# Norm factors of the second mixer moved behind the output projection, in one kernel of a four-mixer block

## The chip, the cores and the metric

The kernel runs on one core of a Trainium2 chip. The metric is the device time of one execution in microseconds; lower is better.

## The reference

One block of a model: `x` (512 tokens x 1024) is normalised, projected by `w_in`, and the projected columns feed four mixers whose outputs, 512 channels each, are concatenated and projected back by `w_out`. Cut to what matters here, the second mixer (a chunked state-space mixer) ends with a norm over each of two groups of 256 channels:

```
h = _rmsnorm(x, norm_g[l])
p_fox, p_ssm, p_nsa, p_mem = _split(h @ w_in[l], ...)
...
yg = (y * jax.nn.silu(z)).reshape(B, S, SSM_GROUPS, GROUP_W // SSM_GROUPS)
return _rmsnorm(yg, norm_g.reshape(SSM_GROUPS, -1)).reshape(B, S, GROUP_W)
...
o = jnp.concatenate([fox, ssm, nsa, mem], axis=-1)
x = x + o @ w_out[l]
return _rmsnorm(x, final_norm_g)
```

`_rmsnorm` multiplies each token's group by `rsqrt(mean(y*y) + EPS)`, one factor for each token and group, and by a gain for each channel.

## The kernel before

All matrix products that need full precision are split in two float32r parts, high and low, and computed as three matmuls (`three`): high by high, high by low, low by high. Weights come from HBM in 75 tiles of 128x1024 in the order of the table `ORDER` (line 53): `load` issues the DMA of a tile into a ring of three buffers (`raw`), `split` makes its high part on ACT (`wh`) and its low part on DVE or POOL (`wl`), and `get` hands both to the matmuls.

Two kinds of work alternate on TensorE. The background is a list of generators in `ORDER`: projections of 128 columns (`tile_a`, eight steps of three matmuls of 512 columns, after a first step that only takes the weights), then a "sink" that moves the result out of PSUM with several ACT and DVE instructions. The pipes are the mixers (`fox`, `ssm`, `nsa`, `mem`, and the small `prep` and `cmp`), each cut into stages. Which goes when is written out by hand in the string `PLAN` (line 67): `.3` is three background steps, `L0` issues the next weight DMA, `W0` splits the next weight tile, `O1` splits one output tile of mixer 1, and a letter with a number is the next stage of a pipe (`f0` is the first stage of fox, `s4` the fifth of ssm). The string sets the order of instructions on each engine; semaphores set the times. `PICKS` says for each instruction that could go to several engines which one takes it (V DVE, A ACT, P POOL).

The second mixer works channel-major: in its stage `s3` a chunk of 128 tokens is a tile `yc` of 128 channels by 4x128 tokens, and its squares go to `sq`. `s4` sums the squares over channels with a matmul against ones (tile `pn`) and takes the power -1/2 on POOL (`rsr`), which gives a factor for each token in the partition direction. `s5` turns the factors into rows over all partitions with two fp32 matmuls against the identity (`bcast_rows`, tile `prs`) and multiplies `yc` by the gain and the rows into `of` with four DVE instructions. Later `split_o` makes the high and low parts `oh` and `ol`, and `out_proj(1, c)` multiplies them by the weights `wo1`: for each pair of token tiles it sums all four channel tiles f = 0 to 3 in one PSUM tile `po` for each token tile, and one DVE addition for each token tile brings the sum into `acc`. A loop over c covers the two halves of the 1024 outputs. The same function serves mixers 0 and 2; the last, mixer 3, has `out_last`, followed by the final norm.

PSUM has eight tiles of 128x512 for everything (`PS`). Every `PS` tile is taken again once its readers are done.

Of the kernel before, what the change touches and what calls it, by code (L numbers as in the profile page):

```python
# [67 lines left out]
    "p0.9W0.8L0.5W0.2L0p1W0.7L0L0.2W0.9L0L0.6W0.6W0f0f0f0.6L0L0.3f1.6W0.1W0.5f0L0.4f1.6W0f1.3L0f1L0.6W0.3"  # L68
    "f2.5L0.1f3.1f0f2f0f0f2.3W0W0f2.4f3f1.2f1.4f2f2f4.5f3.1f3W0f0f4f0L0.6f4.2f5.1f1L0.3f3.1W0L0.4W0f4f1f0"
    "f2f0f1.6L0L0.5f3f3.6W0W0f0.2f1f1f2.1f2.2f4f4.1W0f3f3s0.1f4f1f4f0f0f0f1f1f1f4f2f2.2f3.5L0L0.4f5f2f2.1"  # L70
    "f2f3f2.4W0W0.6f4L0L0f0L0f3c0.1W0.3f5.1f3f5f5f5f3.5W0.9.1f4f4f5.4f4f4O0f1f5f5L0.1s0s0.3L0f2s1s1.5W0.2"
# [1 line left out]
    "W0s3B0B0B0.2L0.3s4L0s4s4.1B0.1W0.9.6W0W0s5s5s5n0n0.7L0.2L0n1.3W0W0.2L0L0L0n0n1n0.1n1.3n2n2n2.8n1W0n3"
    "n0.1n1W0.5n2W0L0n3n4n4n2.4n0n0n3n5n5n3L0.8n1n1W0L0n4n0.2O1O1.2n2.3n3.3n2.2W0.1n3n0.1n0n0n1n1.3O1.3L0"
    ".1L0.3n2W0W0n5.2n1n1n0n0n4n4n4.4L0.1n2W0O1.7n1n1n3n4n2n2n3n3n2n0L0.2n3n3n0n5.5W0n5n3n2.4L0.1n5n3n0n4"
    "n4.1n5n5.4n0n1n4n4n0L0n1n1W0n2n0n2n4.3n1.1n2.3n5L0.4W0.3n5.4n2W0n5n5.3n1n1n3n0n0n0.8L0L0.1n3W0n2n1n1"
    ".4n3n3n3.3n1n4n4n4n4.1W0n5n2W0n5n5n5n0n0n0n0.3n1.1n4.1n2n2.1n2.2L0n3.3W0.9n3.1n1n3.2B0n4n4.2n0L0L0n2"
    ".3L0n4.1n4n1W0n1n2n5n5n3.1W0.2n5.3n0n0n3n1n3.8n2.1n0.3n0W0L0L0n2.5n2n1n5n1n4n4n4n3n1W0n3n3n0n2.2n2n1"
    "n4n4.1n3.3n4W0.9n2.3L0m0m0L0m0.2W0L0.3W0.2n1m1n5m1n5n5n5n4m1n2.2n5n5O2n5n3n3m2.1n2W0.4m2.1m3.1m2.1m3"
    "m3m4n4m0m0m0m0n5m4m4n3n5.1n3.1m5m5O2m1m1n4.1n4m2L0n4n5n5m2L0m1m3m6n5L0m2m5O2O2m3m3m0.2m4.1W0.4m4.5W0"  # L80
    "m4.3m5m5m5m1m1m2W0m6m6m2m3m3.1L0.1L0.3m4m4L0.2m6.4W0.4m6m6.1m5m5.1W0.2m6m6.2W0.9.9.9.9.1"
# [4 lines left out]
    "M": "VAAAVVVA",  # L86
    "Rk": "AVVAAVVV",
    "Rl": "VAAAAAVA",
    "ce": "PPVVVV",
    "ct": "AVAAVAVVAAVAVVVA",  # L90
    "kh0": "AVV",
    "kh1": "AVV",
    "ll": "PVPVPPVV",
    "m": "PVVPVPVV",
# [2057 lines left out]
```

## Time and profile before

| | |
|---|---|
| median of 3 runs | 511.45 us (511.14 to 514.05) |
| the profiled execution | 511.3 us, of which the span from first to last instruction is 509.5 us |
| TensorE (PE) busy | 496.4 us, 97% of the span, 2965 matmuls |
| DVE, ACT, POOL busy | 368.9, 297.3 and 164.4 us |
| mean granted TensorE clock | 0.997 |

A busy time counts how long instructions of the engine lasted; a matmul's record lasts longer than the distance to the next one, since matmuls are pipelined. So what a matmul takes of the engine's time is read from the distance of the starts of neighbours. An idle time is named after what ended it.

### The profile page before, as it was taken

How to read it: one execution, taken by the hardware profiler on the slowest of the kernel's cores; microseconds unless marked ns; L12 is line 12 of the kernel's file. 1: busy time of each engine (PE TensorE's matmuls, PEld its weight loads, DVE VectorE, ACT ScalarE, POOL GpSimd, SP SyncE). 2: the span in 40 equal slices, each digit the busy share in tenths (PEclk: the TensorE clock that was granted, in tenths of full speed). 3: DMA queues.
4: the chain of work that ended last, by engine and by line, in shares of the span. 5: the costliest groups of instructions: out<-in, count | busy, mean ns of one | idle time of the engine just before them, and what ended most of it. 6: DMA issues, size and time to landing. Idle time of an engine off the chain costs nothing.

```text
span 509.5 us, 8995 instructions
## 1 busy us (share of the span) xinstructions
PE 496.4 (97%) x2965; PEld 419.6 (82%) x2965; DVE 368.9 (72%) x981; ACT 297.3 (58%) x671; POOL 164.4 (32%) x113
## 2 busy tenths in 40 slices
PE   8999999989999999999899999999999999999995
PEld 5898877877788888888788888788888898898884
DVE  5486686667678688997988786787777786655644
ACT  5856366777545535664464776755756654664343
POOL 3594303030133103643653132340251220521532
PEclk9999999999999999999999999999999999999998
DMA  8791824526687679444345477777766776832213
GB/s 300 314 326 53 93 85 144 183 79 170 155 262 214 194 228 373 130 171 170 132 152 172 123 225 198 238 219 213 197 196 212 233 233 163 255 138 83 84 41 124
DMA packets 72446, 92.66 MB, mean 182 GB/s; under 512 B 26784, under 2 KB 50624, under 8 KB 72400
## 3 DMA queue, kind: packets, MB, share of 16 engines
q1 hardware_dynamic: 71968, 91.51, 58.5%
q10 hardware_dynamic: 432, 0.59, 0.3%
q8 instruction: 23, 0.38, 0.3%
q14 instruction: 23, 0.19, 0.1%
HBM read 73.68 MB, written 20.55 MB: 185 GB/s over the span
## 4 chain that ended last, share of the span: by engine, by line
PE 56%; DVE 19%; ACT 9%; DMA 6%; issue 5%; SPq 2%; POOL 2%; POOLq 0%; ACTq 0%; DVEq 0%
PE pj L360 25%; PE po L360 10%; PE pb L360 7%; PE pO L360 5%; PE pS L360 4%; ACT pN L360 3%; DMA raw<-in_wst 3%; DVE wl L360 2%; DVE fl L360 2%; SPq L360 2%; DVE pN L360 1%; DVE xs L360 1%; ACT pF L360 1%; DMA far<-fl 1%; DVE rs L360 1%
## 5 line engine op out<-in xcount | busy, mean ns | idle before, releaser
L360 POOL TENSOR_TENSOR wl<-raw,wh 128x1024 fp32r<-128x1024 f32 (+1 forms) x44 | 109.3, 2493 | 258.9 <-ACT wh L360 182.9
L360 PE MATMUL pj<-hh,wl 128*128 128x512 f32 x352 | 137.6, 391 | 3.5 <-POOL wl L360 2.8
L360 PE MATMUL pj<-hh,wh 128*128 128x512 f32 x352 | 138.5, 393 | 0.5 <-ACT wh L360 0.5
L360 PE MATMUL pj<-hl,wh 128*128 128x512 f32 x352 | 137.2, 390 | 0.0
L360 PEld LDWEIGHTS pj<-hh,wl 128*128 128x128 f32 x352 | 66.1, 188 | 19.1 <-POOL wl L360 3.6
L360 ACT ACTIVATE wh<-raw 128x1024 fp32r<-128x1024 f32 (+1 forms) x72 | 73.3, 1034 | 8.5 <-DMA raw<-in_wst 3.4
L360 PEld LDWEIGHTS pj<-hh,wh 128*128 128x128 f32 x352 | 66.1, 188 | 14.7 <-ACT wh L360 0.9
L360 PEld LDWEIGHTS pj<-hl,wh 128*128 128x128 f32 x352 | 66.1, 188 | 13.0
L360 ACT ACTIVATE pN<-pN,nm 128x128 f32<-128x128 f32 (+7 forms) x96 | 45.3, 473 | 37.5 <-DVE nm L360 36.3
L360 DVE TENSOR_TENSOR wl<-raw,wh 128x1024 fp32r<-128x1024 f32 (+1 forms) x29 | 37.8, 1310 | 4.6 <-ACT wh L360 4.1
L360 PE MATMUL po<-wh,oh 128*128 128x512 f32 x96 | 37.7, 393 | 0.0
L360 PE MATMUL po<-wh,ol 128*128 128x512 f32 x96 | 37.5, 390 | 0.0
L360 PE MATMUL po<-wl,oh 128*128 128x512 f32 x96 | 37.5, 390 | 0.0
L360 ACT ACTIVATE pF<-pF,nm 128x128 f32<-128x128 f32 (+3 forms) x32 | 17.8, 556 | 28.3 <-DVE nm L360 27.4
L360 DVE TENSOR_TENSOR acc<-acc,po 128x512 f32<-128x512 f32 (+1 forms) x33 | 21.1, 663 | 9.9 <-PE po L360 9.8
L360 DVE STREAM_TRANSPOSE fl<-pN 128x128 f32<-128x128 f32 (+3 forms) x64 | 27.9, 482 | 0.1
L360 DVE SCALAR_TENSOR_TENSOR rs<-sm,gat 128x3 f32<-128x3 f32 x32 | 6.6, 206 | 28.8 <-ACT pN L360 28.8
L360 ACT ACTIVATE pN<-pN,rs 128x128 f32<-128x128 f32 (+3 forms) x31 | 16.1, 544 | 12.9 <-DVE rs L360 12.9
L360 DVE CUSTOM_DVE_ANT_0 pN<-pS,bt 128x128 f32<-128x128 f32 (+5 forms) x80 | 22.1, 320 | 0.1
L360 DVE SCALAR_TENSOR_TENSOR xs<-x,cwh,xs 128x512 f32<-128x512 f32 x24 | 19.0, 790 | 4.0 <-ACT xs L360 3.4
L360 PEld LDWEIGHTS po<-wh,ol 128*128 128x128 f32 x96 | 18.0, 188 | 3.8
L360 PEld LDWEIGHTS po<-wl,oh 128*128 128x128 f32 x96 | 18.0, 188 | 3.6
(273 smaller groups left out, 1009.2 us busy)
## 6 DMA issues: line engine op xcount, KB each, us to landing
raw<-in_wst SPq DMA_DIRECT2D x73, 512.0 KB, 5.0
far<-fl SPq DMA_DIRECT2D x144, 64.0 KB, 2.1
pt<-far SPq DMA_DIRECT2D x36, 256.0 KB, 3.9
far<-fl SPq DMA_DIRECT2D x96, 48.0 KB, 1.7
pt<-far SPq DMA_DIRECT2D x24, 192.0 KB, 2.9
rows<-rv SPq DMA_DIRECT2D x4, 656.0 KB, 7.1
bt<-rows SPq DMA_DIRECT2D x4, 528.0 KB, 4.9
xn<-in_xn SPq DMA_DIRECT2D x4, 512.0 KB, 7.2
```

Of the source, the lines that this page charges most:

```text
L360: return f(*a, **k)
```

## The change

Stage `s5` of the second mixer is gone. `s4` writes its factors into a fixed tile `rn` (128 tokens by 4 chunks x 2 groups) and multiplies `yc` by the gain alone into `of`, in one instruction of 128x512 for each chunk, on the engine that `PICKS` names. In `out_proj(1, c)` the two groups of channels are summed apart: the matmuls of f = 0, 1 form one PSUM sum and those of f = 2, 3 another, and each is scaled by its column of `rn` and added into `acc` by one DVE instruction (`scalar_tensor_tensor`). The tables `ORDER`, `PLAN` and `PICKS` are new throughout; all tiles and stages but `s5` are in both. The diff, with `ORDER` whole and of `PLAN` and `PICKS` the lines that are spoken of:

```diff
 ORDER = (
-    ("bv", 0), ("bv", 1), ("bv", 2), ("bv", 3), ("bc", 0), ("bc", 1), ("bc", 2), ("fq", 0), ("xb", 6),
-    ("fk", 1), ("xb", 3), ("xb", 0), ("fk", 0), ("kc", 0), ("fk", 3), ("fk", 2), ("fq", 1), ("fq", 3),
-    ("fq", 2), ("fg", 0), ("vc", 0), ("xb", 1), ("z", 2), ("xb", 5), ("fg", 2), ("z", 3), ("xb", 7), ("fg", 3),
-    ("xb", 4), ("fg", 1), ("xb", 2), ("z", 1), ("z", 0), ("kw", 0), ("nq", 0), ("wo0", 0), ("wo0", 1),
-    ("ks", 0), ("nq", 2), ("mv", 0), ("mv", 1), ("mv", 2), ("mv", 3), ("nq", 1), ("mg", 3), ("wo0", 2),
-    ("wo0", 3), ("ng", 0), ("ng", 2), ("ng", 1), ("wo1", 0), ("wo1", 1), ("mk", 3), ("nq", 3), ("ng", 3),
-    ("wo1", 2), ("wo1", 3), ("mq", 0), ("mg", 0), ("mk", 2), ("mk", 0), ("mg", 1), ("mk", 1), ("mq", 1),
-    ("mq", 2), ("mq", 3), ("mg", 2), ("wo2", 2), ("wo2", 3), ("wo2", 0), ("wo2", 1), ("wo3", 0), ("wo3", 1),
+    ("bv", 0), ("bv", 1), ("bv", 2), ("bv", 3), ("bc", 0), ("bc", 1), ("bc", 2), ("xb", 6), ("fq", 0),
+    ("z", 3), ("xb", 3), ("fg", 0), ("fk", 0), ("xb", 0), ("kc", 0), ("fq", 3), ("fq", 1), ("fk", 2),
+    ("fk", 1), ("z", 2), ("xb", 1), ("fq", 2), ("z", 1), ("fk", 3), ("fg", 2), ("vc", 0), ("fg", 1), ("xb", 5),
+    ("xb", 7), ("xb", 4), ("xb", 2), ("fg", 3), ("nq", 0), ("z", 0), ("kw", 0), ("wo0", 0), ("wo0", 1),
+    ("nq", 2), ("ks", 0), ("mv", 0), ("mv", 1), ("mv", 2), ("mv", 3), ("nq", 1), ("ng", 0), ("wo0", 2),
+    ("wo0", 3), ("ng", 2), ("mg", 3), ("ng", 1), ("mk", 3), ("wo1", 0), ("wo1", 1), ("nq", 3), ("wo1", 2),
+    ("wo1", 3), ("ng", 3), ("mq", 2), ("mk", 1), ("mg", 0), ("mq", 3), ("mq", 0), ("mk", 0), ("mk", 2),
+    ("mq", 1), ("mg", 1), ("mg", 2), ("wo2", 0), ("wo2", 1), ("wo2", 2), ("wo2", 3), ("wo3", 0), ("wo3", 1),
     ("wo3", 2), ("wo3", 3),
 )
...
 PLAN = (
...
-    "f5W0.2f5f5f3f3s2f5c1f4f5s3f4f5B0f5O0c2O0W0.1O0s1.9.3s0L0W0.3s2s2c3s3L0s3.2L0L0.5s4s1.9.2W0W0.3s2L0s5"
...
+    "L0p0.9.1W0.9.1W0.6L0.3L0L0.8W0W0L0.4W0.2L0.9.4W0.3p1f0L0f0f0f0.9.1f1f1W0.7f2L0f2s0.1f3.2f1W0W0L0.2L0"
+    "L0.2f2.3f0.2f4.3f1.3f2W0.1f3f3.1f2f4O0.2f3.1f5.1f5f5.1f1.7L0.3L0f2f5f3f2.1f5.2f5f4f5f3W0.1W0.2f3.1W0"
+    "c0f4.5s0.8s1s1f5f4f4L0L0f5f5.5f4W0c1s2.1s0f5c2O0s2L0O0O0s1.9L0W0.1s3s3c3W0s2.6s3s4B0s4s1.2W0.6s2.3L0"
+    ".2W0.3s3.3B0B0L0W0.5B0B0.5L0.1L0.1W0.3L0.7W0s4s4W0n0.2L0n1L0L0.4W0.4W0n0n0.6n2L0.3L0n1n1n2n2.3O1.3W0"
+    ".3L0n2n5.1W0n3W0.2n2n2n1n1O1W0n0n3.2B0n1.2n2.4n0L0L0n2.7n1.2n3.4n5n5.1n2n5n3W0n4n4n4L0L0n1n4n2W0n3n3"
+    "n5n1.2n3.2n1n4L0.7m0m0.3n5.3n4.2W0n1m0m0n2n2m0n4n4n3n3m1m1n5n5n5n5m2m2W0m1.8m3m3m2m1.1m4O2n4.1O2O2n2"
...
 PICKS = {
...
-    "pF": "VVVVVVVAVAVVVVAVAAVVVVVAAVVVAVVV",
-    "pN": "AVVVAAVVAVAAAAVAVAVAVAAAVVVVVAAVAAVAVVAAAVVVAVAVAAAVAVVAVVAAVVVV",
-    "xde": "VVV",
-    "xp": "VVPVVVVV",
-    "yc": "PVVVVVVVVVVPVVVP",
+    "of": "VPVV",
+    "pF": "AAAVVVVVAAAAVVAAVAAVAAVAVVAVVAVV",
+    "pN": "VAAAAVAAAVAAVAAAAAAVAVAVVAAVVAAVAAVVAAVAAVAVVVVVVAVAVAAAVAAAVVAV",
+    "xde": "VPV",
+    "xp": "PPPVPVVP",
+    "yc": "PPVPVVVVPPVPPPPV",
...
@@ -530,7 +531,7 @@
 
 CONSTS = {"ones": [128, 128], "umask": [128, 128], "vcm": [96, 128], "w2": [128, 2, 64], "sp": [128, 4, 16],
           "nv": [128, 4, 296], "dA": [128, 32], "cst": [128, 776], "nhalf": [128, 8], "cbh": [128, 8], "rx": [128, 4],
-          "gat": [128, 4, 24], "x0": [128, 632], "cwh": [128, 32], "nacs": [128, 32],
+          "rn": [128, 8], "gat": [128, 4, 24], "x0": [128, 632], "cwh": [128, 32], "nacs": [128, 32],
           "dte": [128, 32], "decR": [128, 32]}
 
 
@@ -1088,6 +1089,8 @@
         tk = slice(f * 128, (f + 1) * 128) if mixer == 1 else slice(t * 128, (t + 1) * 128)
         three(p, (hi[:, tk], lo[:, tk]), (w_[0][:, cs], w_[1][:, cs]), f == ends[0], f == ends[1], 512)
 
+    rn = C1("rn")
+
     def out_proj(mixer, c):
         if not acc:
             load_acc()
@@ -1099,7 +1102,7 @@
                 for x in range(2):
                     t = 2 * t2 + x
                     for f in (2 * i, 2 * i + 1):
-                        first = f == (0 if t2 == 0 else 2)
+                        first = f % 2 == 0 if mixer == 1 else f == (0 if t2 == 0 else 2)
                         hi, lo = o_hl[mixer, t if mixer == 1 else f]
                         yield max(clock.ready([hi, lo, *w_[i]]), clock.free_banks(1) if first else 0.0)
                         if first:
@@ -1107,10 +1110,16 @@
                                 p = []
                             p.append(PS("po"))
                         cs = slice(f % 2 * 512, f % 2 * 512 + 512)
-                        out_mm(p[x], mixer, t, f, w_[i], cs, (0, 3) if t2 == 0 else (2, 1))
+                        out_mm(p[x], mixer, t, f, w_[i], cs,
+                               (2 * i, 2 * i + 1) if mixer == 1 else (0, 3) if t2 == 0 else (2, 1))
                 if t2 == 1:
                     done(w_[i])
-            for x in range(2):
+                for x in range(2) if mixer == 1 else ():
+                    t = 2 * t2 + x
+                    a = acc[t][:, 512 * c:512 * c + 512]
+                    V.scalar_tensor_tensor(out=a, in0=p[x], scalar=rn[:, 2 * t + i:2 * t + i + 1], in1=a,
+                                           op0=OP.mult, op1=OP.add)
+            for x in range(2) if mixer != 1 else ():
                 a = acc[2 * t2 + x][:, 512 * c:512 * c + 512]
                 V.tensor_tensor(out=a, in0=a, in1=p[x], op=OP.add)
         if c:
@@ -1796,21 +1805,12 @@
             for g in range(2):
                 T.matmul(pn[:, g:g + 1], sq[:, g * 256:g * 256 + 128], ones[:, 0:1], start=True, stop=True)
             gs.drop()
-            st[c] = (yc, rsq(pn[:, 0:2], 2, 1.0 / 256, "rs"))
-
-        def s5(c):
-            yc, r = st.pop(c)
-            pr = PS("prs")
-            bcast_rows(pr, r, 2)
+            rsq(pn[:, 0:2], 2, 1.0 / 256, "rs", rn[:, 2 * c:2 * c + 2])
             of = o_f[1, c] = G("of")
-            for j in range(4):
-                jc, gc = slice(j * 128, (j + 1) * 128), slice(j // 2 * 128, (j // 2 + 1) * 128)
-                V.scalar_tensor_tensor(out=of[:, jc], in0=yc[:, jc], scalar=v_sg[:, j:j + 1], in1=pr[:, gc],
-                                       op0=OP.mult, op1=OP.mult)
+            tt(0, out=of.rearrange("p (j l) -> p j l", j=4), in0=yc.rearrange("p (j l) -> p j l", j=4),
+               in1=v_sg[:, :, None].to_broadcast([128, 4, 128]), op=OP.mult)
             gs.drop()
-            if LAST == 1:
-                split_o(1)
-                last[0] = c + 1
+            del st[c]
             if c == 3:
                 gs.drop(12)
                 for j in range(4):
@@ -1826,7 +1826,7 @@
         def p3(c):
             return [("z", j) for j in range(4)], lambda: []
 
-        return Pipe(list(range(4)), [s0, s1, s2, s3, s4, s5], DS, [0, 3, 1, 1, 1, 1], [(1, 0), lambda c: (max(2, (5, 7, 7, 5)[c] - RS), 0), (1, 0), (2, 0), (0, 0), (3 if LAST == 1 else 1, 0)], RS,
+        return Pipe(list(range(4)), [s0, s1, s2, s3, s4], DS, [0, 3, 1, 1, 1], [(1, 0), lambda c: (max(2, (5, 7, 7, 5)[c] - RS), 0), (1, 0), (2, 0), (0, 0)], RS,
                     {0: p0, 1: p1, 3: p3}, (3,))
 
     def mem_r():
```

## Rows read from the trace of the kernel before

**Rows 1.** The page: busy time and share of the span of each engine, and of the view in 40 equal slices the busy tenths of TensorE and the clock it was granted.

```profile
PE 496.4 (97%) x2965; PEld 419.6 (82%) x2965; DVE 368.9 (72%) x981; ACT 297.3 (58%) x671; POOL 164.4 (32%) x113
...
PE   8999999989999999999899999999999999999995
...
PEclk9999999999999999999999999999999999999998
```

**Rows 2.** The view of waits, TensorE alone: tile waited with, tile and engine waited for, us in total, times, the longest.

```profile
PE pj L360 <- POOL wl L360: 2.8, 2, 1.5
...
PE pO L360 <- ACT ct L360: 0.8, 1, 0.8
PE pj L360 <- DVE wl L360: 0.5, 1, 0.5
PE pj L360 <- ACT wh L360: 0.5, 1, 0.5
```

**Rows 3.** The view by windows: for each stretch its length, then the busy us and instructions of PE, PEld, DVE, ACT and POOL, the granted clock, the DMA share, GB/s.

```profile
100.00:120.00 20.00, 18.48 (x87) 15.26 (x86) 15.59 (x29) 13.94 (x23) 4.99 (x2) 1.00 0.32 99
...
240.00:250.00 10.00, 8.72 (x39) 6.88 (x38) 8.85 (x14) 7.67 (x15) 4.78 (x4) 1.00 0.33 130
250.00:260.00 10.00, 10.00 (x76) 8.59 (x75) 8.30 (x22) 1.87 (x3) 5.55 (x4) 1.00 0.48 157
260.00:270.00 10.00, 10.00 (x53) 8.59 (x52) 8.94 (x20) 6.80 (x9) 7.16 (x6) 1.00 0.74 211
...
320.00:340.00 20.00, 19.98 (x136) 17.06 (x137) 15.95 (x58) 12.67 (x34) 8.66 (x6) 1.00 0.75 221
```

**Rows 4.** The timeline of TensorE around the matmuls that go and around three waits: start, us, operation, output and inputs, shapes, count, and in brackets idle time before and what ended it. Neighbouring rows of one kind are the steady stream.

```profile
112.36 0.39 PE L360 MATMUL pj<-hh,wh 128*128 128x512 f32 x1
112.59 0.39 PE L360 MATMUL pj<-hl,wh 128*128 128x512 f32 x1
114.50 0.50 PE L360 MATMUL pj<-hh,wl 128*128 128x512 f32 x1 [1.52 <-POOL wl L360]
...
126.49 0.39 PE L360 MATMUL pj<-hh,wl 128*128 128x512 f32 x1
127.35 0.50 PE L360 MATMUL pj<-hh,wh 128*128 128x512 f32 x1 [0.47 <-ACT wh L360]
127.69 0.40 PE L360 MATMUL pj<-hl,wh 128*128 128x512 f32 x1
128.61 0.50 PE L360 MATMUL pj<-hh,wl 128*128 128x512 f32 x1 [0.53 <-DVE wl L360]
...
247.92 0.39 PE L360 MATMUL pj<-hl,wh 128*128 128x512 f32 x1
249.59 0.51 PE L360 MATMUL pj<-hh,wl 128*128 128x512 f32 x1 [1.28 <-POOL wl L360]
249.93 0.61 PE L360 MATMUL prs<-cst,rsr 128*128 128x128 f32 x4
250.47 0.44 PE L360 MATMUL pY<-m,xdt 128*64 128x128 f32 x4
...
266.82 1.50 PE L360 MATMUL prs<-cst,rsr 128*128 128x128 f32 x12
268.07 0.38 PE L360 MATMUL pS<-kh,L 128*128 128x288 f32 x1
```

**Rows 5.** Groups of instructions by operation and shape: output and inputs, shapes, count, busy us and mean ns of one, idle time before.

```profile
L360 POOL TENSOR_TENSOR wl<-raw,wh 128x1024 fp32r<-128x1024 f32 x42 | 106.2, 2538 | 250.7 <-ACT wh L360 174.6 <-PE pO L360 24.1 <-DVE ql L360 16.8
L360 ACT ACTIVATE wh<-raw 128x1024 fp32r<-128x1024 f32 x69 | 71.6, 1052 | 8.5 <-DMA raw<-in_wst 3.4 <-issue 1.7 <-POOL rx L360 1.4
...
L360 DVE TENSOR_TENSOR wl<-raw,wh 128x1024 fp32r<-128x1024 f32 x27 | 36.4, 1357 | 4.6 <-ACT wh L360 4.1
L360 DVE TENSOR_TENSOR acc<-acc,po 128x512 f32<-128x512 f32 x31 | 20.3, 679 | 9.9 <-PE po L360 9.8
...
L360 DVE SCALAR_TENSOR_TENSOR xt<-xt,x,pr 128x512 f32<-128x512 f32 x7 | 5.0, 735 | 0.0
...
L360 DVE SCALAR_TENSOR_TENSOR of<-yc,x,prs 128x128 f32<-128x128 f32 x16 | 4.3, 342 | 0.0
```

**Rows 6.** The view of single tiles, engines other than TensorE: operation, count, ns min/median/max, first and last start, shapes. Tiles `m`, `yc`, `xp`, and the small `rs` of the softmaxes.

```profile
L360 SPq DMA_DIRECT2D m<-acd x8: 320/432/642, 160.8 to 219.2; - x8
...
L360 DVE TENSOR_TENSOR m<-m,umask x5: 672/683/693, 203.8 to 243.4; 128x512 f32<-128x512 f32 x5
L360 POOL TENSOR_TENSOR m<-m,umask x3: 1285/1715/2272, 195.1 to 222.3; 128x512 f32<-128x512 f32 x3
...
L360 POOL TENSOR_TENSOR yc<-yc,sg x3: 461/787/844, 215.6 to 254.0; 128x128 f32<-128x128 f32 x3
...
L360 POOL TENSOR_TENSOR xp<-xst,x x1: 752/752/752, 166.6 to 166.6; 128x248 f32<-128x248 f32 x1
...
L360 DVE SCALAR_TENSOR_TENSOR rs<-sm,gat x32: 161/164/1410, 273.1 to 421.7; 128x3 f32<-128x3 f32 x32
```

**Rows 7.** The timeline of ACT and of POOL ahead of the wait at 112.59 us, columns as in rows 4.

```profile
104.90 0.72 ACT L360 ACTIVATE pF<-pF,nm 128x512 f32<-128x512 f32 x1 [4.07 <-DVE nm L360]
...
110.95 1.04 ACT L360 ACTIVATE wh<-raw 128x1024 fp32r<-128x1024 f32 x1
...
112.07 2.37 POOL L360 TENSOR_TENSOR wl<-raw,wh 128x1024 fp32r<-128x1024 f32 x1 [8.54 <-ACT wh L360]
```

More of the change, by code (lines that the diff above doesn't have):

```diff
@@ L67 @@
 PLAN = (
[L68 to L71, printed above, removed]
-    "f5W0.2f5f5f3f3s2f5c1f4f5s3f4f5B0f5O0c2O0W0.1O0s1.9.3s0L0W0.3s2s2c3s3L0s3.2L0L0.5s4s1.9.2W0W0.3s2L0s5"
@@ L73 @@
[L73 to L81, printed above, removed]
+    "L0p0.9.1W0.9.1W0.6L0.3L0L0.8W0W0L0.4W0.2L0.9.4W0.3p1f0L0f0f0f0.9.1f1f1W0.7f2L0f2s0.1f3.2f1W0W0L0.2L0"
@@ new lines @@
+    "f1.7L0.2W0s0.9.2f2L0.2W0.6f0f3f0f0f3W0.9f4.2f1L0.4f1f1f2f2f2W0W0f0f1.5f3.1f3L0L0.1f2.1f2.5f0f0W0f0f4"
+    "f4f4f1f5f5f5f5f1f2.5f0.6L0.1f1.6f4W0f0.4L0f5f3f2f3.1f1f4f4.1f3.1W0W0.1f3.2f1.1L0L0f0f0f2.3f4f4W0f3f1"
+    "L0.2f2.3f0.2f4.3f1.3f2W0.1f3f3.1f2f4O0.2f3.1f5.1f5f5.1f1.7L0.3L0f2f5f3f2.1f5.2f5f4f5f3W0.1W0.2f3.1W0"
+    "c0f4.5s0.8s1s1f5f4f4L0L0f5f5.5f4W0c1s2.1s0f5c2O0s2L0O0O0s1.9L0W0.1s3s3c3W0s2.6s3s4B0s4s1.2W0.6s2.3L0"
+    ".2W0.3s3.3B0B0L0W0.5B0B0.5L0.1L0.1W0.3L0.7W0s4s4W0n0.2L0n1L0L0.4W0.4W0n0n0.6n2L0.3L0n1n1n2n2.3O1.3W0"
@@ new lines @@
+    "W0.1n3n3n0n0.6W0.6n1n1n0n4n0.4n4n3n1L0n4n2.5n1L0.1L0W0W0n2.4n3n3.1n2n0n0n0n4n0n0n1.1O1.3n1.9.3O1n4L0"
+    ".3L0n2n5.1W0n3W0.2n2n2n1n1O1W0n0n3.2B0n1.2n2.4n0L0L0n2.7n1.2n3.4n5n5.1n2n5n3W0n4n4n4L0L0n1n4n2W0n3n3"
+    "n0n3n0n3n0.1n1.2n5n5n5.3n4.2W0n5.2n1.6n5n2n2.1n3.1n0n0n2W0.1n1.2L0.2n2n4.4n1n1n3n4n4n4L0n2n0n0.3L0n2"
+    "n3.4n1n1W0n3n2.6n3W0n0n0n5n3L0.5n4n5.2n5n5.2n1n3L0.2W0W0.4n5n1n0n0n0n2n2n3n4n4n4L0n4n4.1n3n2.2n1n1.5"
+    "W0.1n5.5L0n0n1n0L0.6W0.3W0.1n0.2n2n1n1n1n2n2n3n2.3n5W0.5n4n3n3.6n0n2n3.2L0.1n5n5L0.2n0n0W0n4n4n3n4n5"
@@ L82 @@
+    "n5n1.2n3.2n1n4L0.7m0m0.3n5.3n4.2W0n1m0m0n2n2m0n4n4n3n3m1m1n5n5n5n5m2m2W0m1.8m3m3m2m1.1m4O2n4.1O2O2n2"
+    "n2m3n3n3m0m2m5m0L0L0m4m5.1m6n5n5n5m1m4n4n4n4W0m3n5n5m1m2m3n5.1n5.2m2m1m4m4m3m5m5m5O2m2m4m0m6m6m5m3.2"
+    "m6.5W0L0L0L0.1m4.4m6.2W0.1m6W0.2L0.5m1.6m2m3m4.4m5m5L0W0W0m6m6W0.9.9.9.9.2"
 )
 PICKS = {
[L86 to L94, printed above, removed]
@@ L95 @@
-    "ml": "PVPV",
-    "ol": "VVPVPPVPVPPVPPV",
-    "pF": "VVVVVVVAVAVVVVAVAAVVVVVAAVVVAVVV",
-    "pM": "VAAVVVAAVAVVVAVA",
-    "pN": "AVVVAAVVAVAAAAVAVAVAVAAAVVVVVAAVAAVAVVAAAVVVAVAVAAAVAVVAVVAAVVVV",
-    "sq": "VPVPVPPV",
-    "wl": "PVPPPPPPPPPPVVVPVPVPPVVVPPPVPPVVPVVPVPPVPVPPVVPVPPVPPPPVVPPPPPVPVPVPPPVV",
-    "xde": "VVV",
-    "xp": "VVPVVVVV",
-    "yc": "PVVVVVVVVVVPVVVP",
+    "M": "VAAVVAVA",
+    "Rk": "VVVVVVAV",
+    "Rl": "AAVAAAAV",
+    "ce": "VPVPVV",
+    "ct": "VAAVAAVAAVVAVVVV",
@@ L105 @@
+    "kh0": "VVA",
+    "kh1": "VAV",
+    "ll": "VVPVPPVV",
+    "m": "VVVVPVVV",
+    "ml": "PVPP",
+    "of": "VPVV",
+    "ol": "VPVPPVPPVPPVPVP",
+    "pF": "AAAVVVVVAAAAVVAAVAAVAAVAVVAVVAVV",
+    "pM": "AAVAVVAAVVAAVAVA",
+    "pN": "VAAAAVAAAVAAVAAAAAAVAVAVVAAVVAAVAAVVAAVAAVAVVVVVVAVAVAAAVAAAVVAV",
+    "sq": "PPVPVPPP",
+    "wl": "PVPPPPPPPPVPVPVPVPPVVVVVPPPVVPVVVVVVPPVPVPVPVPPPPPPVVPPPPPPPPPPVPPPPVVVP",
+    "xde": "VPV",
+    "xp": "PPPVPVVP",
+    "yc": "PPVPVVVVPPVPPPPV",
 }
```

## The prediction

> **What bounds the kernel.** I read the page first. TensorE is busy 97% of the span, in nearly all 40 slices 9 tenths, and it is granted its full clock (the level of 2.4 GHz) in all but the last slice [rows 1]. DVE at 72% is next. A share that high can still hide waits, since a matmul's record is longer than its turn, so the second view is the waits of TensorE alone: inside the kernel it stood idle 2.8 + 0.8 + 0.5 + 0.5 = 4.6 us, nearly all of it for the low part `wl` of a weight tile [rows 2]. Third, the windows: around the second mixer TensorE is busy 10.00 of 10 us in two stretches and 8.72 in one, and in the stretch from 100 it has 18.48 of 20 [rows 3]. Fourth, the timeline, which gives what one matmul costs the stream: neighbours start 0.23 us apart (112.36, 112.59), though each is written down with 0.39 [rows 4]. It also gives what a wait costs, as distance of starts less 0.23: at 112.59 it is 114.50 - 112.59 - 0.23 = 1.68 us, at 126.49 0.63, at 127.69 0.69 and at 247.92 1.44, together 4.4 us [rows 4]. So the time is TensorE's work plus a few us of waits. The change can win by less work on TensorE, and by an order with smaller waits; it can lose only by new waits, because no matmul is added.
>
> **What goes from TensorE.** Eight calls in the code, two rows each in the trace, are 16 matmuls into `prs`. The first four take 250.47 - 249.93 = 0.54 us until the next kind starts, the other twelve 268.07 - 266.82 = 1.25 us [rows 4]. Sum 1.8 us. It is on the path: TensorE is full on both sides [rows 3]. `out_proj` for mixer 1 issues the same matmuls as before, only with other marks for the start of a sum, and the 582 background steps of `PLAN` are the same number: 0.
>
> **What goes to and from the other engines.** DVE loses 16 x 0.342 = 5.5 us (`of`) [rows 5]. For `of` it gets three, POOL one, of 128x512 with a broadcast input. No such instruction is in the trace; the masked `m` has the same form: 0.683 on DVE, 1.715 on POOL [rows 6], so 2.0 and 1.7 us. The eight additions into `acc` of 0.679 become 16 scaled ones. Bounds for one: 0.679 (the addition) and 0.735 (a scaled product that reads a column, SBUF and PSUM) [rows 5]; I take 0.735, the same operation: 11.8 against 5.4, so +6.3. DVE's balance is -5.5 + 2.0 + 6.3 = +2.8 us. Against it `PICKS` moves eight of the `pF` and six of the `pN` scalings from DVE to ACT. All this costs nothing as long as TensorE has other matmuls. The cover of the scaled additions is local: a pair of token tiles and one group is 12 matmuls, 12 x 0.23 = 2.8 us, and two additions empty the pair in 1.5 us, so two more PSUM tiles fill while two are emptied. Without that cover, that is if DVE's queue is already late, it costs up to the whole 6.3 us.
>
> The factors still go through DVE and POOL in `s4`, but no matmul and no `of` waits for them now; the first who needs `rn` is a scaled addition in the third quarter of the kernel. The DMAs of the first two `s0` stages are put ahead in SP's queue, among fox's transfers: four issues of 0.43 us, 1.7 us [rows 6]. Queued behind them are weight loads. Bounds 0 to 1.7; I take 0, since no wait of TensorE in rows 2 ended with a DMA.
>
> **What the order does to the waits.** For each weight tile I counted in `PLAN` the background steps between its `W0` and the step that takes it; a step is three matmuls, 0.68 us. A tile needs 1.05 us on ACT and then 1.36 on DVE or 2.54 on POOL [rows 5], and only the third matmul of the first step with work needs the low part. The mean distance is 11.4 steps before and 11.3 after, so the new order isn't looser on the whole. What differs is where the short ones lie.
> - `ks` was split one step ahead, on POOL (`s1.9.2W0W0.3`). That is the 1.44 us at 247.92. In the new plan it is 13 steps ahead: -1.4.
> - The waits at 112 to 129, 1.68 + 0.63 + 0.69 = 3.0 us, aren't short distances: the first tile was split 12 steps ahead. They come from sinks: ACT stood 4.07 us waiting for DVE, its copy of the weights began at 110.95 and POOL's part at 112.07 [rows 7]. `ORDER` had five tiles with heavy sinks in a row there (`fk` 3, `fk` 2, `fq` 1, `fq` 3, `fq` 2). The new one has four (`fq` 3, `fq` 1, `fk` 2, `fk` 1), then the light `z` 2, split 18 steps ahead, and `xb` 1 at 16 steps instead of 8. Bounds: nothing gained, or 3.0. I take half, -1.5, since the sinks are the same instructions.
> - New tight places: `fg` 3 at 3 steps (`W0.1W0.2f3`) and `mk` 3 at 2 (`W0n3W0.2`), both on DVE; `mg` 2 at 1 step on POOL, but with three `m0` between. Idle engines need 1.05 + 1.36 = 2.4 us against 3 or 2 steps, 2.0 and 1.4, plus 0.45: nearly met. With engines as late as at 112.59 each costs up to 1.7. Bounds 0 to 5.0; I take 0.6, nearer to nothing because `nq` 1, split one step ahead on DVE before, has no wait of that size beside the four above.
> - `f0L0f0f0f0`: four fox stages in a row want eight PSUM tiles while the projection `kc` holds a ninth, so the fourth waits for DVE to read the first. Bounds 0 and, with the largest wait seen, 1.7; I take 0.6.
>
> Sum: -1.4 - 1.5 + 0.6 + 0.6 = -1.7 us.
>
> **Total.** 511.3 us for the profiled execution (span 509.5 and 1.8 around it), less 1.8, less 1.7: 507.8 us. The median of the runs is 0.15 above that execution, which I leave out.
>
> **A rule that speaks against it.** One small DVE instruction of 0.16 us took 1.41 once, and POOL's `m` lies between 1.3 and 2.3 us [rows 6]: the two engines hold each other up. Behind it stands the Trainium skill, SBUF — State Buffer, section "Who interferes with whom": a DVE instruction with two inputs in SBUF and a GpSimd one that reads SBUF exclude each other for a whole instruction. By that rule the old `of`, with one input in PSUM, was free of it, and the new one isn't; rows 6 agree in kind. What it would cost is the fourth rival.
>
> **The rivals.**
> 1. *The saved time turns into waiting.* The matmuls go, but the sinks keep TensorE waiting as before and the new tight places eat what `ks` gives back. For: mean distances equal. Against: TensorE is full from 250 to 270 [rows 3], so what follows moves up. Time between 511.3 - 1.8 = 509.5 and 513: with the upper bounds of the new waits 511.3 - 1.8 - 1.4 + 5.0 = 513.1.
> 2. *All the waits of rows 2 go.* 511.3 - 1.8 - 4.6 = 504.9. For: a `wl` wait is only a question of order. Against: ACT and DVE carry the same sinks.
> 3. *DVE becomes the last in the output projection of mixer 1*, slower than before: PSUM tiles aren't emptied in time. 511.3 - 1.8 + 6.3 = 515.8. It decides once DVE, busy 15.95 of 20 us from 320 [rows 3], has less than 6.3 us free over the time in which the projection runs. Against: 4.05 us are free in each 20, the projection is spread over more than that, and 14 scalings went to ACT.
> 4. *POOL holds DVE in the second mixer.* Moved to POOL: six `yc` x 0.787, four `xp` x 0.752, one `of` and one `xde` of 1.7 each, 11.1 us [rows 6]. If DVE stood for all of it with no free time, 511.3 - 1.8 + 11.1 = 520.6; DVE has 1.2, 1.7 and 1.1 us free in the three stretches of ten from 240 [rows 3], so most of it is absorbed, and some 516 to 519 is what a bad case leaves. The point is the first time that an `m` or `yc` comes late for a matmul.
>
> **Chances.** One per cent is 5.1 us, about what a measurement of this kernel can tell from no change. Forecast (506.3 to 509.5): 0.43. Rival 1 (509.5 to 513): 0.30. Rival 2 (504 to 506.3): 0.14. Rival 3 (513 to 516): 0.08. Rival 4: 0.05. Faster by over 1%, under 506.2: rival 2 nearly whole and the edge of the forecast, 0.17. Slower by over 1%, over 516.6: rival 4 and little else, 0.05. Within 1%: 0.78. The range for 8 in 10 runs from 504.8, where the lower half of rival 2 is cut off, to 514.0, which leaves out rival 4 and most of rival 3.
>
> **What would show it.** Right: 2949 matmuls, no `prs`; no wait at `ks`; the sum of TensorE's waits near 3 us; `of` with three rows near 0.68 on DVE; the scaled additions near 0.735 with TensorE not waiting ahead of `po`. Wrong: waits of TensorE on `wl` of `fg` 3 or `mk` 3, on fox's `pS` at the four stages in a row (rival 1), on `po` (rival 3), or on `m` and `yc` tiles (rival 4). A granted clock under full speed in a stretch would upset the whole sum.

## The result and the profile after

The changed kernel takes 508.3 us (median of 5 runs, 508.07 to 508.63) where the kernel before takes 511.9 beside it (511.14 to 514.05); the ratio is 0.9925, 95% interval 0.9902 to 0.9949. Run again in another comparison it took 508.85 against 512.03, ratio 0.9935 (0.9921 to 0.9949). That is 3.2 to 3.6 us less; forecast were 507.8 and 3.5 less than the profiled execution. One remark on the comparisons: in that of the first four experiments the kernel before took 511.8 to 512.3 us in eight runs and 513.7 to 516.4 in fifteen; there I compare with the eight, 511.9, while the recorded ratios are to the median of all 23, 514.4.

The page after, lines as in [rows 1]:

```profile
PE 495.0 (98%) x2949; PEld 417.2 (82%) x2949; DVE 361.0 (71%) x951; ACT 303.2 (60%) x684; POOL 166.5 (33%) x126
...
PEclk9999999999999999999999999999999999999999
```

16 matmuls are gone, and the work has moved from DVE (7.9 us less) to ACT (5.9 more) and POOL (2.1 more). The waits of TensorE after, columns as in [rows 2] (1.3 us more stand ahead of the first product, in both kernels):

```profile
PE pj L361 <- DVE wl L361: 1.3, 2, 0.8
PE pT L361 <- DVE nm L361: 1.1, 2, 0.9
PE pW L361 <- DVE sg L361: 1.0, 1, 1.0
PE pj L361 <- ACT wh L361: 0.5, 1, 0.5
```

3.9 us against 4.6 (the view of before has two more, of 0.4 and 0.3 us, that [rows 2] leave out). They are not the old waits made smaller; they are other ones. The timeline of TensorE after, columns as in [rows 4]:

```profile
64.66 0.39 PE L361 MATMUL pj<-hh,wl 128*128 128x512 f32 x1
65.59 0.50 PE L361 MATMUL pj<-hh,wh 128*128 128x512 f32 x1 [0.54 <-ACT wh L361]
65.93 0.40 PE L361 MATMUL pj<-hl,wh 128*128 128x512 f32 x1
66.85 0.50 PE L361 MATMUL pj<-hh,wl 128*128 128x512 f32 x1 [0.53 <-DVE wl L361]
...
194.31 0.40 PE L361 MATMUL pj<-hl,wh 128*128 128x512 f32 x1
195.49 0.50 PE L361 MATMUL pj<-hh,wl 128*128 128x512 f32 x1 [0.78 <-DVE wl L361]
...
290.77 0.39 PE L361 MATMUL pS<-kl,L 128*128 128x512 f32 x1
292.16 0.44 PE L361 MATMUL pW<-kh,L 128*128 128x384 f32 x1 [1.00 <-DVE sg L361]
...
295.15 0.39 PE L361 MATMUL po<-wh,ol 128*128 128x512 f32 x1
296.44 0.29 PE L361 MATMUL pT<-cst,pcp 128*96 128x128 f32 x1 [0.90 <-DVE nm L361]
```

By distance of starts less the turn of the matmul before (0.23 for 512 columns, less for fewer) these cost 0.70, 0.69 (both `fg` 0), 0.95 (`fg` 3), 1.16 and 1.06, with 0.34 at 307.9 together 4.9 us. Of before the same reading gives 6.7: the 4.4 of [rows 4], and 2.3 in four smaller ones, two at 82 to 83 and one each at 319 and 355, which I hadn't counted. The last matmul starts 3.0 us earlier than before, and from there to the end it is 6.5 us in both, so all of the difference lies in the stream of matmuls. By this account it is 1.8 us of waits, the 1.8 of the removed matmuls, and 0.6 back that no listed gap explains (0.13 of it ahead of the first projection, which starts at 41.71 instead of 41.58).

The output projection of mixer 1, where DVE got more to do, shows no wait. Windows after, columns as in [rows 3]:

```profile
320.00:340.00 20.00, 20.00 (x153) 17.55 (x152) 17.00 (x49) 11.83 (x27) 10.09 (x8) 1.00 0.80 239
340.00:360.00 20.00, 20.00 (x102) 16.60 (x103) 15.35 (x61) 11.57 (x36) 2.53 (x2) 1.00 0.64 181
360.00:380.00 20.00, 20.00 (x137) 17.07 (x134) 15.78 (x62) 13.77 (x37) 7.41 (x5) 1.00 0.81 243
```

And the new operations, view of the tiles `of` and `acc`, columns as in [rows 6]:

```profile
L361 DVE TENSOR_TENSOR of<-yc,x x3: 682/684/883, 238.7 to 266.8; 128x512 f32<-128x512 f32 x3
L361 POOL TENSOR_TENSOR of<-yc,x x1: 1037/1037/1037, 240.8 to 240.8; 128x512 f32<-128x512 f32 x1
...
L361 DVE SCALAR_TENSOR_TENSOR acc<-po,rn,acc x16: 709/742/751, 333.0 to 371.2; 128x512 f32<-128x512 f32 x16
```

0.684 and 0.742 us were forecast as 0.683 and 0.735; POOL's `of` took 1.04 instead of 1.7.

### The profile page after: what moved, and what is told of

Read it like the earlier page. It is cut to its first block, busy times and chain, and to the rows that moved or that the text cites. A ratio compares the mean times of both kernels' runs of the same rounds, so it can differ in the third digit from the quotient of the medians.

```text
span 506.5 us, 8961 instructions
## 1 busy us (share of the span) xinstructions
PE 495.0 (98%) x2949; PEld 417.2 (82%) x2949; DVE 361.0 (71%) x951; ACT 303.2 (60%) x684; POOL 166.5 (33%) x126
## 4 chain that ended last, share of the span: by engine, by line
PE 49%; DVE 8%; ACT 5%; issue 2%; DMA 2%; SPq 1%; POOLq 0%; POOL 0%; DVEq 0%; ACTq 0%
PE pj L361 20%; PE po L361 15%; PE pO L361 6%; PE pS L361 3%; ACT pN L361 2%; DVE xs L361 2%; DVE fl L361 1%; PE pY L361 1%; SPq L361 1%; PE pT L361 1%; PE pW L361 1%; DMA raw<-in_wst 1%; DMA far<-fl 1%; DVE wl L361 1%; DVE rs L361 1%
## 5 line engine op out<-in xcount | busy, mean ns | idle before, releaser
L361 POOL TENSOR_TENSOR wl<-raw,wh 128x1024 fp32r<-128x1024 f32 (+1 forms) x44 | 105.0, 2393 | 200.0 <-ACT wh L361 171.7
L361 DVE TENSOR_TENSOR wl<-raw,wh 128x1024 fp32r<-128x1024 f32 (+1 forms) x29 | 36.0, 1250 | 4.4 <-ACT wh L361 4.2
L361 ACT ACTIVATE pN<-pN,rs 128x256 f32<-128x256 f32 (+3 forms) x37 | 19.2, 541 | 16.6 <-DVE rs L361 16.6
L361 DVE SCALAR_TENSOR_TENSOR rs<-sm,gat 128x3 f32<-128x3 f32 x32 | 7.9, 245 | 29.3 <-ACT pN L361 29.3
L361 DVE TENSOR_TENSOR acc<-acc,po 128x512 f32<-128x512 f32 (+1 forms) x25 | 16.1, 660 | 13.5 <-PE po L361 13.5
L361 DVE RECIPROCAL rs<-sm 128x2 f32<-128x2 f32 x24 | 4.0, 166 | 24.3 <-ACT pF L361 15.0
L361 PEld LDWEIGHTS po<-wh,oh 128*128 128x128 f32 x96 | 18.1, 188 | 3.6 <-issue 0.2
```

Of the source, the lines that this page charges most:

```text
L361: return f(*a, **k)
```

## The experiments

**Arithmetic and order apart.** Two kernels, each with one half of the change. The first has the new arithmetic in the order of before:

```diff
 # tables of before; of PLAN only the s5 steps are taken out
-    ".5s4s1.9.2W0W0.3s2L0s5" "W0s3B0B0B0" ... "W0W0s5s5s5n0n0"
+    ".5s4s1.9.2W0W0.3s2L0"   "W0s3B0B0B0" ... "W0W0n0n0"
+    "of": "VPVV",
```

> The new arithmetic (factors behind the projection, groups summed apart) with the old tables: PLAN of before with its four s5 tokens taken out, ORDER and PICKS of before plus the line for of. Theory (the time is TensorE's matmuls plus its waits, and the two parts of the change add): 1.8 us less than before, about 509.8 us, ratio 0.9965, with the wait at ks (1.4 us) and those at 112 to 129 us still in the trace. Rival A (the removed matmuls only turn into waiting; the order makes the gain): no difference from before, ratio 1.000. Rival B (the scaled additions make DVE late in an order not made for them): up to 6.3 us slower than the theory, ratio above 1.005.

Measured: 520.06 us (519.34 to 521.12), 8.2 above the 511.9 (ratio to all 23 runs of before 1.0112, 1.0078 to 1.0145). The profiled execution, 521.11 with a span of 519.3, is one of the two longest. So it is slower by 8 us, with the same arithmetic that is in the faster kernel, and 10 above the theory, more than rival B allowed. Its waits of TensorE, its windows and its timeline on DVE and POOL:

```profile
PE pj L361 <- POOL wl L361: 3.4, 2, 1.9
PE pW L361 <- DVE sg L361: 2.3, 1, 2.3
...
PE pW L361 <- DVE acc L361: 0.9, 1, 0.9
...
PE po L361 <- DVE nm L361: 0.7, 1, 0.7
```

```profile
250.00:255.00 5.00, 4.32 (x34) 3.73 (x35) 3.11 (x4) 0.00 (x0) 3.93 (x2) 0.66 0.57 188
...
370.00:375.00 5.00, 4.46 (x13) 3.74 (x14) 3.95 (x20) 2.84 (x11) 0.00 (x0) 0.66 0.92 278
```

```profile
366.54 3.22 DVE L361 TENSOR_TENSOR wl<-raw,wh 128x1024 fp32r<-128x1024 f32 x1
...
366.29 2.40 POOL L361 TENSOR_TENSOR wl<-raw,wh 128x1024 fp32r<-128x1024 f32 x1 [14.62 <-ACT wh L361]
```

By distance of starts: the wait for `ks` grew from 1.44 to 2.03 us, two new ones at 269 to 271 cost 1.5, three at 337 to 346, in the output projection, 2.3, and one at 368 costs 2.4. Behind the waits of 2.0 and 2.4 us the granted clock is 0.66 over 5 us, twice 5 x 0.34 = 1.7. Sum 0.6 + 1.5 + 2.3 + 2.4 + 3.4 - 1.8 = 8.4 of the 9.8 us by which the span is longer. So the arithmetic isn't free by itself: in the old order the same stretch doesn't take it without waits. But 4.1 us of the sum, the wait at 368 and the clock behind it, come from one encounter of DVE and POOL, which a later experiment takes out (2.6 us less in the end).

The second has the new order with the old arithmetic:

```diff
 # tables of the changed kernel; functions of before; PLAN with s5 put back
-    ".2W0.6s2.3L0" ... "L0L0.4W0.4W0n0n0"
+    ".2W0.6s2s5s5.3L0" ... "L0L0.4s5s5W0.4W0n0n0"
```

> The old arithmetic (prs matmuls, four scaled products into of, one sum over both groups) with the new tables, stage s5 put back in at two places of the new PLAN, well behind its s4. Theory: the 1.8 us of matmuls come back and the waits stay those of the new order, so about 1.8 us above the changed kernel, 510.1 us, ratio to before 0.996 to 0.997. Rival A: as fast as the changed kernel, 508.3 us. Rival B: faster than the changed kernel, as DVE loses the eight extra additions.

Measured: 511.1 us (510.68 to 513.24), span 508.9; 0.8 below before's 511.9, and 2.4 in span above the changed kernel. Of these 0.7 are a difference in waits (5.5 against 4.9 us by distance of starts), which leaves 1.7 for the 16 matmuls and their surroundings. One wait is new, 1.44 us at 274.93 for a `wl` that DVE began behind POOL's; the waits at `fg` 0 and `fg` 3 and those behind 290 are there with the old arithmetic too. The new one on DVE and POOL:

```profile
273.82 2.72 DVE L361 TENSOR_TENSOR wl<-raw,wh 128x1024 fp32r<-128x1024 f32 x1
...
273.06 2.39 POOL L361 TENSOR_TENSOR wl<-raw,wh 128x1024 fp32r<-128x1024 f32 x1 [2.19 <-ACT wh L361]
```

Run once more, unchanged, the changed kernel gave 508.85:

> The changed kernel once more, unchanged, beside the three that follow and on the same chip as they. All theories: 508 to 510 us, the more of it the longer the wait at 65 us (0.7 us in its first profile, 2.0 us in two other kernels with this order on another chip).

So the four corners are: before 511.9; order alone 511.1; arithmetic alone 520.1 (517.6 once the encounter at 366 is taken out, below); both 508.3 to 508.9.

**Was the wait at `ks` a matter of distance?** First the split of `ks` 11 steps earlier in the kernel before (12 ahead of its use and not 1), at the end of stage `s1`:

```diff
-    ... ".5s4s1.9.2W0W0.3s2" ...
+    ... ".5s4s1W0.9.2W0.3s2" ...
```

> The kernel before with one token of PLAN moved: the split of the weight tile ks stands 12 background steps ahead of its use and not 1. Theory (that wait is a short distance and nothing else): the wait of 1.4 us at 248 us is gone and the time is 1.4 us less than before, about 510.2 us, ratio 0.997. Rival (ACT, DVE and POOL are late there whatever the order): the wait moves to a later tile, ratio 1.000.

Measured: 514.19 us against 514.39 for all runs of before, ratio 0.9992 (0.9963 to 1.002), and the wait is still 1.44 us, at 248.27. Its timeline on ACT says why (columns as in [rows 7]):

```profile
243.84 2.45 ACT L360 ACTIVATE m<-m,nacs 128x128 f32<-128x128 f32 x8 [1.20 <-DVE m L360]
246.21 3.10 ACT L360 ACTIVATE wh<-raw 128x1024 fp32r<-128x1024 f32 x3
```

Between the two places of the split no instruction is issued on ACT. The copy `wh` stood behind the eight exponentials `m` of `s1`, which waited for DVE, in either case. Then the split one step further, ahead of `s1`:

```diff
-    ... ".5s4s1.9.2W0W0.3s2" ...
+    ... ".5s4W0s1.9.2W0.3s2" ...
```

> The kernel before, with the weights of the second mixer's ks placed ahead of step s1, so that their copy on ACT (wh) comes ahead of the exponentials ce and m of that step on ACT's instruction stream; nothing else is changed. Theory: the wait of 1.44 us at 248.3 comes from what stands ahead of wh on ACT and not from the distance to its matmul; then the wait goes, with no new one of over 0.5 us near it, and the time is 1.0 to 1.4 us below the kernel before beside it. Rival: the next thing behind it, the weights' transfer or the step s1 itself, is then as late, the wait stays or moves to s1, and the time is the same within 0.5 us.

Measured: the wait at `ks` is gone, and the kernel is slower, 516.87 us against 513.44 beside it, ratio 1.0071 (1.005 to 1.0091). The timeline of this kernel on DVE, POOL and TensorE:

```profile
251.25 3.19 DVE L360 TENSOR_TENSOR wl<-raw,wh 128x1024 fp32r<-128x1024 f32 x1
...
251.00 2.37 POOL L360 TENSOR_TENSOR wl<-raw,wh 128x1024 fp32r<-128x1024 f32 x1 [2.62 <-ACT wh L360]
...
259.98 0.61 PE L360 MATMUL pn<-ones,sq 128*128 128x1 f32 x4 [2.72 <-POOL sq L360]
```

POOL's next `wl` now starts 0.25 us ahead of one on DVE, which takes 3.19 us and not the 1.23 it takes alone; the `yc` and `sq` behind it come late, TensorE stands 2.72, and the granted clock is 0.66 from 260 to 265. -1.4 + 2.9 + 1.7 = +3.2, of 3.4 by the medians; the profiled execution, 515.38, is the shortest of the six, which run up to 518.57, so the sum is rough. The theory was right on where the old wait came from and wrong on its price: what stands ahead on ACT decided the one, what stood behind it on POOL the other.

**The waits of the new order.** `fg` 3, one of the places I had named, split 13 steps earlier in the changed kernel (`.7`, `.3`, `.1` and `.2` lie between):

```diff
-    "...f5f5.1f1.7L0.3L0f2f5f3f2.1f5.2f5f4f5f3W0.1W0"
+    "...f5f5.1f1W0.7L0.3L0f2f5f3f2.1f5.2f5f4f5f3.1W0"
```

> The changed kernel with one token of PLAN moved: the split of the weight tile fg 3 stands 13 steps ahead of its use and not 3, so that DVE makes its low part ahead of three long products of a convolution. Theory: the wait of 0.95 us at 194 us is gone, about 507.4 us, 0.998 of the changed kernel, ratio to before 0.991. Rival (DVE is full around 194 us, 17.0 of 20 us): its three products come late instead, the wait moves to another tile, and the time stays at 508.3 us.

Measured: 507.46 us (507.14 to 507.69), span 505.6 against 506.5: the wait at 194 is gone, and its 0.9 us are the time. Next the waits at `fg` 0. In the changed kernel SP's queue shows the cause, with the store `rmd` of the memory's norm factors ahead of the weights' loads; it waits 11 us for POOL's `rmr`:

```profile
51.87 0.39 SPq L361 DMA_DIRECT2D rmd<-rmr  x1
52.37 5.83 SPq L361 DMA_DIRECT2D raw<-in_wst  x3
```

The kernel of the experiment before, with that store issued just ahead of its load at 227 us:

```diff
-        Q.dma_start(out=rmd.rearrange("t p -> p t"), in_=r)   # in mem_r
+        return r
...
-    def prep_mem():
+    def prep_mem(r):
+        Q.dma_start(out=rmd.rearrange("t p -> p t"), in_=r)
```

> The changed kernel with the weights of fg 3 earlier (507.46 us before), and with the store of the memory's norm factors (rmd) moved from 52 us to just ahead of its load at 227 us, so that the weights' loads on SP's queue no longer stand 11 us behind it. Theory: the waits at 64.7 and 65.9 (0.7 us each) come from this queue; they go, and the time is 1.2 to 2.2 us below the changed kernel, for fg 3 and fg 0 together, plus up to 1.3 us more where the chip shows the longer wait at 65. Rival: the loads wait for their buffers and not for the queue; then only fg 3's 0.9 us is gained.

Measured: 506.08 us (505.82 to 507.35), 2.8 below the changed kernel beside it (2.1 by the spans), ratio to before 0.9887 (0.987 to 0.9903). SP's queue in this kernel:

```profile
43.29 25.41 SPq L361 DMA_DIRECT2D raw<-in_wst  x5
```

The first load is issued at 43.29 instead of 52.37, and of the 1.4 us at `fg` 0 there is 0.26 left. Both waits were of the order and not of the arithmetic (the new order has them with the old arithmetic too), and both could be taken out by moving one thing. This is the fastest kernel of the study.

**How much more could DVE take in the output projection?** Each of the 16 scaled additions doubled (the second adds 0 times the group), and then 4 of them:

```diff
                     V.scalar_tensor_tensor(out=a, in0=p[x], scalar=rn[...], in1=a, op0=OP.mult, op1=OP.add)
+                    V.scalar_tensor_tensor(out=a, in0=p[x], scalar=0.0, in1=a, op0=OP.mult, op1=OP.add)
+                    # second kernel: only if t == 1
```

> The changed kernel, with each of its 16 scaled additions followed by a second one of the same shape that adds 0 times the same group of channels: 16 more instructions of 0.74 us, 11.8 us more of DVE between 333 and 372; the output is not changed by them. Theory: in the output projection of the second mixer TensorE is last, and DVE has some 1.3 us free in each 2.8 us of matmuls (a pair of 256-row halves), so doubling takes DVE to about as much as TensorE; the time goes up by 0 to 2 us. Rival: DVE is last there, and the time goes up by most of the 11.8 us, 6 to 12.

Measured: 521.73 us against 513.44 of before, ratio 1.0159 (1.0143 to 1.0175). The changed kernel did not run beside it. By the spans it is 520.6 - 506.5 = 14.1 us longer than the changed kernel. Of this 2.9 us lie far ahead of the doubled additions: 1.2 at `fg` 0, where this chip shows 1.92 us in place of 0.70, and 1.7 behind it, where the granted clock is 0.66 from 68 to 73; the wait at `fg` 3 comes 2.95 us later than in the changed kernel. That leaves 11.2 us for 16 x 0.692 = 11.1 us of DVE (with a constant factor an addition takes 0.692 us, with the column of `rn` 0.742). The rival is right. TensorE waits for `acc`, and its clock falls:

```profile
PE pS L361 <- DVE acc L361: 1.4, 2, 0.8
PE pW L361 <- DVE acc L361: 1.4, 2, 0.7
```

```profile
370.00:380.00 10.00, 8.46 (x68) 6.94 (x64) 8.77 (x27) 3.71 (x12) 2.49 (x2) 0.83 0.44 132
```

> The changed kernel with 4 of its 16 scaled additions doubled (one of each four), 2.8 to 3.0 us more of DVE between 333 and 372, about what the change itself added to DVE (2.8 us); the output is not changed. Theory: DVE has some microseconds of reserve in this stretch, which the doubling of all 16 used up; then the time is 0 to 1 us above the changed kernel beside it. Rival: each microsecond more of DVE in this stretch is a microsecond of the whole, as the doubling of all 16 cost 12 to 13 us for 11.1 us; then 2.5 to 4 us above.

Measured: 510.66 us (510.08 to 511.66) against 508.85, 1.8 more for 4 x 0.69 = 2.8 us of DVE. Its profile shows three new waits, 0.32 at 353.7, 0.77 at 360.3 and 0.39 at 376.2, 1.5 together. Two of them end with a `wl` of POOL, one with `nm` on DVE. (The 12 to 13 us that the expectation names for the doubling of all 16 hold the 1.7 us of clock at 68; it is 11.) Neither theory holds whole: about 1 us of reserve is left, and the rest is paid for.

**DVE behind POOL.** Three kernels change the engine of one `wl` each. In the kernel before, and then in the one with the new arithmetic in the old order, a `wl` of (`wo1`, 2) goes from DVE to POOL:

```diff
-    "wl": "...PPVPPPPVVPPPPPVPV..."
+    "wl": "...PPVPPPPVPPPPPPVPV..."
```

> The kernel before, with one copy of the low weights (wl of wo1, 2) on POOL in the place of DVE, so that DVE and POOL no longer start a wl together at 360.6. Theory: the kernel before has two times (about 511.8 and 515.5) because of which of the two engines comes first there; then all executions lie within 1 us of each other, between 511 and 513, and no stretch near 365 to 370 has half the granted clock. Rival: the two times come from something else; then some executions still lie near 515.

Measured: 513.29 us against 513.44, ratio 0.9994 (0.9977 to 1.0011). Inconclusive for the two times: in this comparison the kernel before had 15 of 17 runs within 1.2 us itself, so there was little to take away, and one of the twelve runs without the encounter still took 516.56, as the rival has it.

> The new arithmetic in the order of before (520.06 us before), with one copy of the low weights (wl of wo1, 2) on POOL in the place of DVE, so that DVE doesn't stand behind POOL at 366.5. Theory: of the 9.8 us that this kernel is longer than before, 2.4 us are the wait at 367.9 and 1.7 us the half clock behind it, both from that encounter; then 515.5 to 517. Rival: the additions on DVE make the same products late without it; then the wait stays over 1 us and the time above 518.

Measured: 517.6 us (517.28 to 518.5) against 520.06 (on another chip), ratio to before 1.0112 (1.0095 to 1.0129); the span is 2.8 us shorter. The wait of 2.4 us and the half clock behind it are gone, 4.1 us; two waits at 374 and 377, of 0.65 and 1.04 us, take back 1.7. The forecast was 515.5 to 517; a part of the theory, since the additions are late there without the encounter as well. What is left, 5.6 us over the kernel before beside it, is the price of the arithmetic in the old order without this encounter.

The third tries to take out the waits at 290 to 296. The timeline of the changed kernel on DVE and POOL ahead of them:

```profile
285.60 2.23 DVE L361 TENSOR_SCALAR pcp<-pN,rs 128x16 f32<-128x16 f32 x1
...
282.92 4.77 POOL L361 TENSOR_TENSOR wl<-raw,wh 128x1024 fp32r<-128x1024 f32 x2
```

An instruction of 0.23 us took 2.23 and ended as POOL's second `wl` ended. So that `wl` (`wo0`, 3) goes to DVE, with `fg` 3 early as above:

```diff
-    "wl": "...PVPVPVPVPPPPPPVVPPPP..."
+    "wl": "...PVPVPVPVPPVPPPVVPPPP..."
```

> The changed kernel with the weights of fg 3 earlier, as in the experiment before (507.46 us), and with one copy of the low weights (wl of wo0, 3) on DVE in the place of POOL, so that POOL makes no second wl while DVE makes pcp at 285.6. Theory: pcp took 2.23 us there because POOL held it, and the waits of 1.16 and 1.06 us at 290.8 and 295.2 stand behind that; then pcp takes well under 1 us, the two waits go to under 0.5 us together, and the time is 505.3 to 506.2. Rival: the wl on DVE (about 1.2 us) delays the same chain as much as POOL did; then the waits stay at about 2 us and the time at 507.0 to 508.0.

Measured: 511.17 us against 513.44 of before, ratio 0.9955 (0.9942 to 0.9968), above both forecasts. By spans 508.9 against the 505.6 of the kernel without this edit; 1.25 of it is at `fg` 0 (this chip again), 2.0 is the edit's own. Its timeline on DVE, POOL and TensorE:

```profile
284.41 2.88 DVE L361 TENSOR_TENSOR wl<-raw,wh 128x1024 fp32r<-128x1024 f32 x1 [0.16 <-ACT wh L361]
...
289.42 0.23 DVE L361 TENSOR_SCALAR pcp<-pN,rs 128x16 f32<-128x16 f32 x1
...
283.81 2.40 POOL L361 TENSOR_TENSOR wl<-raw,wh 128x1024 fp32r<-128x1024 f32 x1
...
294.40 0.44 PE L361 MATMUL pW<-kh,L 128*128 128x384 f32 x1 [2.37 <-DVE sg L361]
```

`pcp` takes 0.23 us, so it was POOL that had held it. But now DVE's `wl` is held by POOL's other one, and all of DVE's queue with it: one wait of 2.5 us and the half clock behind it (1.7) in place of 2.2. I had priced the `wl` at 1.2 us, its time without POOL.

## Why the prediction was right, point by point

The time, the sign and the sum came out, the sum in part by luck. The four terms of the order were forecast as -1.4, -1.5, +0.6 and +0.6; the traces give -1.4, -1.6 (3.0 gone and 1.4 new), +0.95 and 0, and besides +2.6 and -2.3 that I had not foreseen. Both sums are -1.7 to -1.8, but several terms have other reasons than I gave. My first reading of before was also too small: 4.6 us of waits, nearly all for `wl`, are 6.7 by distance of starts, and 3.3 of the 4.6 were for `wl`.

- **The 16 matmuls, -1.8.** Right: 1.7 by the order alone against both, once the difference in waits is taken off.
- **`ks`, -1.4.** The amount is right, the wait doesn't come back in the new order. The reason, a short distance in background steps, is wrong: 11 steps more changed nothing. The copy on ACT stood behind exponentials that waited for DVE.
- **The waits at 112 to 129, -1.5 as half of 3.0.** All 3.0 went, and 1.4 came at `fg` 0, which the new order has moved from place 20 to place 12 and so into the time in which SP's queue is held by a store. The half was right as a net, not as a mechanism. The store moved away, the 1.4 went nearly whole. I had priced the DMAs that are put ahead on SP's queue and taken 0, since no wait of before ended with a DMA; it was one that the change leaves where it was. The kernel before has the same store ahead of the loads, and its profile shows no wait there; but two of its variants, on another chip, do (0.79 and 0.69 us at 65 with `ks` ahead of `s1`, 1.33 and 0.69 with the `wl` on POOL). In the profiles the new order adds 1.0 us: the store goes out at 51.87 instead of 50.87, since POOL's `rmr` takes 1.61 us beside a `wl` on DVE and took 0.71 before. The timeline after, on DVE and POOL, and then before, on POOL:

```profile
50.06 1.22 DVE L361 TENSOR_TENSOR wl<-raw,wh 128x1024 fp32r<-128x1024 f32 x1
...
50.24 1.61 POOL L361 TENSOR_TENSOR rmr<-rmv,nhalf 128x2 f32<-128x2 f32 x1 [6.98 <-DVE rmv L361]
```

```profile
50.13 0.71 POOL L360 TENSOR_TENSOR rmr<-rmv,nhalf 128x2 f32<-128x2 f32 x1 [6.97 <-PE pd L360]
```

- **New tight places, +0.6 of up to 5.0.** `fg` 3 cost 0.95, shown by taking it out; `mk` 3 and `mg` 2 cost nothing.
- **Four fox stages in a row, +0.6.** 0: no wait of TensorE stands there.
- **Not foreseen:** 1.16 + 1.06 + 0.34 at 290 to 308. That POOL's two `wl` in a row hold a small DVE instruction just ahead of them is shown; that the waits come from it is read from the order of DVE's instructions, and no run took all of them away. This is rival 4's mechanism, on another tile and later than I looked; `m` and `yc` were held too (one `m` of 1.77 us) but nothing waited for them. On the other side 2.3 us of small waits of before went as well.
- **DVE's +2.8 at no cost.** True in this order, no wait ahead of `po`. But the reason, that two additions of 1.5 us stand against 2.8 us of matmuls, was too easy: DVE's other instructions in that stretch have to fit too. Some 1 us more is all that fits, and in the old order the change's own share did not (rival 3's mechanism, 2.3 us of the 8.4 there). I had taken arithmetic and order for two terms of a sum. They aren't: -0.8 for the order, +8.2 for the arithmetic (+5.6 without the encounter at 366), and -3.2 to -3.6 together.
- **Granted clock.** It stayed full in the changed kernel, as assumed; in the experiments it added 1.7 us behind each single wait of 2 us and more, and behind some groups of shorter ones.

What stays open: which of the many moves in the tables makes room for the additions in the stretch from 330 to 375, since only whole orders were compared; how much of the two times of the kernel before the encounter at 360.6 makes; and what the waits at 290 to 308 would cost without `pcp` held.
